# SSD outputs computed by channels, the gate listed behind the next group's x, and part of the attention's scaling on another engine

## The chip, the cores and the metric

The kernel runs on one core of one Trainium2 chip. The metric is the device time of one execution in microseconds; the median of the runs is given, and one execution is recorded by the hardware profiler. The engines are called as the profile calls them: PE (TensorE matmul) with PEld (its weight loads), DVE (VectorE), ACT (ScalarE), POOL (GpSimd) and SP (SyncE, which issues the DMAs).

## The reference

One layer of a hybrid decoder, for 256 positions and a model width of 2048, in f32:

```python
a_in = _rmsnorm(h, attn_norm_g[i])
proj = a_in @ w_in[i]
z, xbc, dt_raw, q, k, v = jnp.split(proj, [o1, o2, o3, o4, o5], axis=-1)
xbc = jax.nn.silu(_causal_dwconv(xbc, conv_w[i], conv_b[i]))
...
y = _ssd(xs_h, dt, a_neg, bm.reshape(b, s, SSM_GROUPS, SSM_STATE),
         cm.reshape(b, s, SSM_GROUPS, SSM_STATE))
y = y + d_skip[i].astype(jnp.float32)[:, None] * xs_h.astype(jnp.float32)
y = y.reshape(b, s, SSM_INNER) * jax.nn.silu(z.astype(jnp.float32))
y_ssm = _rmsnorm(y.reshape(b, s, SSM_GROUPS, SSM_INNER // SSM_GROUPS),
                 ssm_norm_g[i].reshape(SSM_GROUPS, SSM_INNER // SSM_GROUPS))
...
y_att = _swa_sinks(qh, kh, vh, sinks[i])
h = h + jnp.concatenate([y_ssm, y_att], axis=-1) @ w_out[i]
u = _rmsnorm(h, ffn_norm_g[i]) @ w_up[i]
u = _causal_dwconv(u, ffn_conv_w[i], ffn_conv_b[i])
g_ff, u_ff = jnp.split(u, [D_FF], axis=-1)
h = h + (jax.nn.silu(g_ff) * u_ff) @ w_down[i]
gate = jax.nn.sigmoid(_rmsnorm(h, ple_norm_g[i]) @ w_ple_gate[i])
pe = _rmsnorm(p[i] @ w_ple_proj[i], ple_post_g[i])
h = h + gate * pe
```

The SSD part has 32 heads of 64 channels in 4 groups; attention has 32 heads, 8 key heads and a window of 128. In `_ssd`, with L = exp of the masked differences of the cumulated decay inside a chunk, the output of a chunk is (C Bᵀ · L) X plus exp(decay) · C · state of the chunk before. There are two chunks (128 positions each), so only the second has a state before it.

## The kernel before

**Products.** Every large product runs in a split form: weights come by DMA in chunks `w` of 128 x 1024 (two k slices of 512 columns), ACT casts the chunk to `wh` (L192), DVE forms the remainder `wl` (L193), and PE multiplies three times (L222 to L224: high by high, low by high, high by low) for each of the two blocks of 128 positions. A chunk is 12 matmuls of 128x512. The sums lie in PSUM as acc pairs, one tile per block, and each of the two tiles has two buffers: a third pair can start only when the first has been read.

**The SSD phase.** A first phase computes B, C and dt (dt's product is copied by ACT to `dtT`, L379, behind a cast and ahead of the evacuations of B, `ct`, L390). Then for each of four groups of 512 channels: `ssd_x` computes x, makes the decay tiles `seg` (128x1024, two per group, broadcast by DMA from `scr`; then subtraction on DVE, mask on POOL, exp on ACT, times C Bᵀ on DVE) and the group's output y by positions (L533: per head one 128x64 matmul; L537: the state's part, scaled on DVE and added). There are three `seg` buffers. `ssd_gate` computes z with Silu. `ssd_end` multiplies, sums squares on ACT, scales by 1/rms (`ry`), transposes `yc` on PE (L272) and splits it into `yT`, the left side of the output projection. `project` (for group 0) or `output` (groups 1 to 3, in the attention phase) multiplies `yT` with its rows of `w_out` in four quarters of 512 columns and adds each acc to the residual `h` on DVE (L397).

**The order.** Each engine works through its own stream in order. In the SSD phase the streams are laid out when the program is built, by a scheduler that starts from the order of the calls in the code; so small products stand between the matmuls of weight chunks. In the attention phase the order on PE is by hand: a list of parts (q, keys, v, outputs) is run chunk by chunk, each a slot, and the table `at` says at which slot `scores` and `values` are issued. `scores` computes masked scores, exp on ACT, the sum `den`, and scales the probabilities `s` by its reciprocal on DVE (L753) before they are transposed by ACT and POOL copies around a DMA transpose.

**Names.** `ms` are two PSUM tiles for small products, `tr` two for transposes; `prev` is the first chunk's state, copied from PSUM by ACT (L527); `rx` is 1/rms of the input.

Of the kernel before, what the change touches and what calls it, by code (L numbers as in the profile page):

```python
# [11 lines left out]
F32 = mybir.dt.float32  # L12
# [53 lines left out]
def hybrid_layer(  # L66
# [251 lines left out]
    with xin_:  # L318
# [59 lines left out]
        V.tensor_copy(rx, rx_)  # L378
        S.copy(dtT, dt_ps[:64, :T])  # L379

# [12 lines left out]

    def add_to_h(acc, n):
        for b in range(NB):
            hs = hres[b][:, n * NC : (n + 1) * NC]
            V.tensor_tensor(out=hs, in0=hs, in1=acc[b], op=ALU.add)  # L397

# [11 lines left out]

    def project(lhs, w, i0, ni, after=None):

        for n in range(4):
            acc = acc_pair()
            gemm(acc, lhs, [w[i, n] for i in range(i0 * KG // KW, (i0 + ni) * KG // KW)])
            add_to_h(acc, n)
            if after:
                after(n)
# [3 lines left out]
    with tc.tile_pool(name="ssd", bufs=1) as sp, tc.tile_pool(name="dram", bufs=1, space=bass.MemoryType.DRAM) as dp:  # L422
        BT = sb(sp, [P, 4, T], "BT")
        CT = sb(sp, [P, 4, T], "CT")
        for c, (acc, dst, tag) in enumerate(((acc_b, BT, "ct"), (acc_c, CT, "Xd"))):
            t = evac_scaled(acc, sp, tag, 1)
            conv_chunk(t, dst, scw, 4, 16 + 4 * c)
            S.activation(out=dst, in_=dst, func=AF.Silu)
# [42 lines left out]
        nc.sync.dma_start(scr, acsT)  # L471
        eacs = sb(sp, [P, 64], "eacs")
        S.activation(out=eacs, in_=acs, func=AF.Exp)

        def ssd_x(g):
            segs = []
            for c in range(NB):
                hs = slice(g * 16 + c * 8, g * 16 + c * 8 + 8)
                seg = sb(sp, [P, 8, P], "seg", bufs=3)
                nc.sync.dma_start(seg, scr[hs, :].partition_broadcast(P))  # L480
                if c == 0:
                    dec = sb(sp, [P, 8], "dec", bufs=2)
                    V.tensor_tensor(out=dec, in0=seg[:, :, P - 1], in1=acs[:, hs], op=ALU.subtract)
                    S.activation(out=dec, in_=dec, func=AF.Exp)
                V.tensor_tensor(out=seg, in0=seg, in1=bc(acs[:, hs], P), op=ALU.subtract)
                G.affine_select(
                    out=seg, in_=seg, compare_op=ALU.is_ge, fill=-1.0e30, base=0, pattern=[[0, 8], [1, P]], channel_multiplier=-1
                )
                S.activation(out=seg, in_=seg, func=AF.Exp)
                segs.append(seg)  # L490
# [19 lines left out]
            S.activation(out=xc, in_=xc, func=AF.Silu)  # L510
            y, Xd = [], []
            for b in range(NB):
                tr = tr_tile()
                for f in range(4):
                    PE.transpose(tr[:, f * P : (f + 1) * P], xc[:, f, b * P : (b + 1) * P], ident)
                yc = sb(sp, [P, NC], f"yc{b}", bufs=2)
                V.tensor_tensor(out=v3(yc, 8), in0=v3(tr, 8), in1=bc(dsk[:, g * 8 : (g + 1) * 8], HD), op=ALU.mult)
                y.append(yc)
# [8 lines left out]
            S.copy(prev, st)  # L527
            for c in range(NB):
                yc = y[c]
                yp = ms_tile()  # L530
                for h in range(8):
                    hs = slice(h * HD, (h + 1) * HD)
                    PE.matmul(yp[:, hs], lhsT=segs[c][:, h, :], rhs=Xd[c][:, hs], start=True, stop=True)  # L533
                V.tensor_tensor(out=yc, in0=yc, in1=yp, op=ALU.add)
                if c:
                    off = ms_tile()
                    PE.matmul(off, lhsT=CT[:, g, c * P : (c + 1) * P], rhs=prev, start=True, stop=True)  # L537
                    t = sb(sp, [P, NC], "xe")
                    o = g * 16 + 8
                    V.tensor_tensor(out=v3(t, 8), in0=v3(off, 8), in1=bc(eacs[:, o : o + 8], HD), op=ALU.mult)  # L540
                    V.tensor_tensor(out=yc, in0=yc, in1=t, op=ALU.add)
            return y

        def ssd_gate(g):
            acc = in_chunk(3 + 2 * g)
            zs = []
            for b in range(NB):
                z = sb(sp, [P, NC], f"z{b}")
                S.activation(out=z, in_=acc[b], func=AF.Silu, scale=rx[:, b : b + 1])
                zs.append(z)  # L550
            return zs

        def ssd_end(g, y, zs):
            ssy = sb(sp, [P, NB], "ssy", bufs=2)
            for b in range(NB):
                V.tensor_tensor(out=y[b], in0=y[b], in1=zs[b], op=ALU.mult)
                S.activation(out=zs[b], in_=y[b], func=AF.Square, accum_out=ssy[:, b : b + 1])
            ry = rstd(ssy, NC, NB, "ry")
            for b in range(NB):
                V.tensor_scalar_mul(y[b], y[b], ry[:, b : b + 1])  # L560
            yT = Lhs(yp_, KG, "y")
            transpose_split(y, yT, 0, g_ssm[:, 4 * g : 4 * g + 4])
            return (yT, w_out, g, 1)

        y = ssd_x(0)
        zs = ssd_gate(0)

# [69 lines left out]
    with tc.tile_pool(name="att_s", bufs=2) as as_, tc.tile_pool(name="att", bufs=2, reuse_waits="tile") as ap_, tc.tile_pool(name="ps_sc", bufs=1, space=PSUM) as ps_sc:  # L637
# [4 lines left out]

        def turned(table, gain, tag):

            t = sb(as_, [P, NB, HALF], tag, bufs=1)
            V.tensor_tensor(out=t, in0=table, in1=gain.unsqueeze(1).to_broadcast([P, NB, HALF]), op=ALU.mult)
            return t


        qa, qc = qscaled[:, :HALF], qscaled[:, HALF:ROPE]  # L650
        qrope = [turned(t, g, f"qr{i}") for i, (t, g) in enumerate(((cos_t, qa), (sin_t, qc), (cos_t, qc), (sin_t, qa)))]
        krope = [cos_t, sin_t, cos_t, sin_t]
        kgain = sb(as_, [P, HD], "kgs", bufs=1)
# [3 lines left out]
        def norm_rope(acc, b, rope, gain=None):  # L657
            r = sb(ap_, [P, NC], "qkr")
            S.activation(out=r, in_=acc[b], func=AF.Copy, scale=rx[:, b : b + 1])
            n = sb(small, [P, NC], "hsq")  # L660
            S.activation(out=n, in_=r, func=AF.Square)
            ss = sb(as_, [P, 8], "ss8")
            V.tensor_reduce(out=ss, in_=v3(n, 8), axis=AX.X, op=ALU.add)
            rs = rstd(ss, HD, 8, "rs8")
            r3 = v3(r, 8)
            V.tensor_tensor(out=r3, in0=r3, in1=bc(rs, HD), op=ALU.mult)
            if gain is not None:
                G.tensor_tensor(out=r3, in0=r3, in1=gain.unsqueeze(1).to_broadcast([P, 8, HD]), op=ALU.mult)
            a, c_ = r3[:, :, :HALF], r3[:, :, HALF:ROPE]
            t = [sb(as_, [P, 8, HALF], f"rot{i}", bufs=1) for i in range(4)]  # L670
            for i, u_ in enumerate((a, c_, c_, a)):
                G.tensor_tensor(out=t[i], in0=u_, in1=rope[i][:, b, :].unsqueeze(1).to_broadcast([P, 8, HALF]), op=ALU.mult)
            G.tensor_tensor(out=a, in0=t[0], in1=t[1], op=ALU.subtract)
            G.tensor_tensor(out=c_, in0=t[2], in1=t[3], op=ALU.add)
            return r
# [45 lines left out]
        def scores(j, b, kvs):  # L721
# [30 lines left out]
            V.reciprocal(den, den)  # L752
            V.tensor_tensor(out=s, in0=s, in1=bc(den, W), op=ALU.mult)  # L753
            p = s.rearrange("p h w -> p (h w)")
# [4 lines left out]
        def values(j):  # L759

            yT = Lhs(yp_, KG, "y")
            for b in range(NB):
# [15 lines left out]
                split(v3(o, 4), hi, lo)  # L778
            held[4 + j] = (yT, w_out, 4 + j, 1)

# [9 lines left out]
        def output(i):  # L790
            lhs, w, i0, ni = held.pop(i)
            for n in range(4):
                acc = acc_pair()
                for s in range(2):
                    products(acc, lhs, load_w(w[i0 * 2 + s, n]), s * KW, KW, KG, s == 1)
                    if s == 1:
                        add_to_h(acc, n)
# [14 lines left out]
        with tc.manual_schedule(engines={PE.engine}):  # L812
            for part in (
                lambda: q(0),
                lambda: chunk(10, keys),
                lambda: chunk(11, load_v),
# [174 lines left out]
```

## Time and profile before

| | |
|---|---|
| median of three runs | 1434.09 us (1433.94 to 1434.67) |
| the profiled execution | 1435.11 us, of which the span in the trace is 1433.4 us |
| DMA | 292.62 MB, mean 204 GB/s |
| weight splits on DVE, L193 | 495 times, 639.8 us in all |
| casts of weights on ACT, L192 | 495 times, 515.0 us in all |
| adds to h on DVE, L397 | 112 times, 72.8 us in all |

An engine's busy time is the sum of its instructions; matmuls overlap in the array, so a matmul's duration (390 ns for a 128x512) is longer than the step from one to the next. Idle time is put down to the event that ended it, behind an arrow: `<-DVE wl L193` is an instruction that waited for DVE's line 193.

### The profile page before, as it was taken

What the parts mean: (1) busy time and instruction counts of PE and PEld (TensorE: products, weight loads), DVE (VectorE), ACT (ScalarE), POOL (GpSimd) and SP (SyncE); (2) the same over time, 40 slices, a digit from 0 to 9 for tenths busy, and PEclk for the clock granted to TensorE, in tenths of its full rate; (3) what the DMA queues carried; (4) which work ended last, traced back from release to release, by engine and by line L of the source; (5) the groups of instructions that cost most, each with busy time, mean ns of one, the idle gap of its engine ahead of it and who ended that gap; (6) DMA issues with size and microseconds to landing.
All of it is one profiled execution on the core that took longest, in us unless ns stands there. A gap on an engine that the chain in (4) does not pass through costs nothing.

```text
span 1433.4 us, 18075 instructions
## 1 busy us (share of the span) xinstructions
PE 1422.4 (99%) x6527; PEld 1166.0 (81%) x6527; DVE 997.2 (70%) x1242; ACT 792.4 (55%) x1069; POOL 290.5 (20%) x234
## 2 busy tenths in 40 slices
PE   9999999999999999999999999999999999999998
PEld 7888888888777777888888888888888888888887
DVE  7678876776789889756667646665675577476854
ACT  6675555645566655556556446545554554455643
POOL 0002010018434422013243113202320131120000
PEclk9999999999999999999999999999999999999999
DMA  9655665557787877568787767867876876776672
GB/s 341 230 175 209 204 182 185 162 160 207 192 224 201 207 208 221 173 203 213 215 231 201 215 203 209 222 200 203 225 209 195 221 217 201 205 208 190 210 224 65
DMA packets 163466, 292.62 MB, mean 204 GB/s; under 512 B 93040, under 2 KB 95920, under 8 KB 162992
## 3 DMA queue, kind: packets, MB, share of 16 engines
q1 hardware_dynamic: 162944, 290.99, 70.1%
q8 instruction: 51, 0.84, 0.3%
q10 hardware_dynamic: 432, 0.48, 0.1%
q14 instruction: 39, 0.32, 0.1%
HBM read 268.32 MB, written 2.13 MB: 189 GB/s over the span
## 4 chain that ended last, share of the span: by engine, by line
PE 65%; DVE 3%; issue 1%; DMA 1%; ACT 0%; DVEq 0%; SPq 0%; ACTq 0%
PE acc L222 21%; PE acc L223 21%; PE acc L224 21%; DVE wl L193 2%; PE tr L769 1%; PE tr L272 0%; PE sc L732 0%; DMA flip<-half 0%; DVE h L397 0%; DVE s L736 0%; DVE nm L743 0%; ACT wh L192 0%; DMA w<-in_w_in_dram 0%; DVE den L751 0%; DVE sg L921 0%
## 5 line engine op out<-in xcount | busy, mean ns | idle before, releaser
L193 DVE TENSOR_TENSOR wl<-w,wh 128x1024 fp32r<-128x1024 f32 (+1 forms) x495 | 639.8, 1298 | 371.5 <-ACT wh L192 370.5
L192 ACT CAST wh<-w 128x1024 fp32r<-128x1024 f32 (+1 forms) x495 | 515.0, 1045 | 488.9 <-PE acc L224 438.1
L223 PE MATMUL acc<-wl,ah 128*128 128x512 f32 x1278 | 499.8, 391 | 0.6 <-DVE wl L193 0.6
L224 PE MATMUL acc<-wh,al 128*128 128x512 f32 x1278 | 498.7, 390 | 0.0
L222 PE MATMUL acc<-wh,ah 128*128 128x512 f32 x1278 | 498.1, 391 | 0.1
L223 PEld LDWEIGHTS acc<-wl,ah 128*128 128x128 f32 x1278 | 240.0, 188 | 51.4 <-DVE wl L193 1.4
L222 PEld LDWEIGHTS acc<-wh,ah 128*128 128x128 f32 x1278 | 240.0, 188 | 51.4 <-issue 1.4
L224 PEld LDWEIGHTS acc<-wh,al 128*128 128x128 f32 x1278 | 239.9, 188 | 50.2 <-issue 0.7
L224 PE MATMUL acc<-wh,gl 128*128 128x512 f32 x352 | 137.0, 389 | 0.0
L223 PE MATMUL acc<-wl,gh 128*128 128x512 f32 x352 | 137.0, 389 | 0.0
L222 PE MATMUL acc<-wh,gh 128*128 128x512 f32 x352 | 136.4, 389 | 0.0
L871 POOL COPY half<-u 128x1024 uint16<-128x1024 uint16 x44 | 60.2, 1379 | 263.0 <-ACT u L869 262.9
L222 PE MATMUL acc<-wh,yh 128*128 128x512 f32 x256 | 101.4, 396 | 0.6 <-DVE h L397 0.6
L223 PE MATMUL acc<-wl,yh 128*128 128x512 f32 x256 | 99.9, 390 | 0.7 <-DVE wl L193 0.7
L224 PE MATMUL acc<-wh,yl 128*128 128x512 f32 x256 | 99.6, 390 | 0.0
L874 POOL COPY uc<-flip 128x1024 uint16<-128x1024 uint16 x44 | 58.8, 1337 | 177.5 <-DMA flip<-half 177.5
L223 PEld LDWEIGHTS acc<-wl,gh 128*128 128x128 f32 x352 | 66.1, 188 | 13.7
L224 PEld LDWEIGHTS acc<-wh,gl 128*128 128x128 f32 x352 | 66.1, 188 | 13.6
L222 PEld LDWEIGHTS acc<-wh,gh 128*128 128x128 f32 x352 | 66.1, 188 | 13.6
L397 DVE TENSOR_TENSOR h<-h,acc 128x512 f32<-128x512 f32 x112 | 72.8, 679 | 1.1 <-PE acc L224 1.1
L288 DVE SCALAR_TENSOR_TENSOR cv<-uc,fcw,cv 128x254 f32<-128x254 f32 (+1 forms) x176 | 73.0, 476 | 0.0
L222 PEld LDWEIGHTS acc<-wh,yh 128*128 128x128 f32 x256 | 48.0, 188 | 14.3 <-issue 3.8
(236 smaller groups left out, 1126.7 us busy)
## 6 DMA issues: line engine op xcount, KB each, us to landing
w<-in_w_up_dram SPq DMA_DIRECT2D x176, 512.0 KB, 4.0
w<-in_w_in_dram SPq DMA_DIRECT2D x126, 512.0 KB, 4.2
w<-in_w_down_dram SPq DMA_DIRECT2D x88, 512.0 KB, 4.2
w<-in_w_out_dram SPq DMA_DIRECT2D x64, 512.0 KB, 4.3
w<-in_w_pg_dram SPq DMA_DIRECT2D x32, 512.0 KB, 4.1
seg<-scr SPq DMA_DIRECT2D x8, 512.0 KB, 5.0
xt<-in_xT_dram SPq DMA_DIRECT2D x16, 128.0 KB, 7.3
h<-in_x_dram SPq DMA_DIRECT2D x2, 1024.0 KB, 8.6
```

The costliest lines, as they stand in the source:

```text
L192: S.copy(hi, src)
L193: V.tensor_tensor(out=lo, in0=src, in1=hi.bitcast(F32), op=ALU.subtract)
L222: PE.matmul(acc[b], lhsT=hi, rhs=wh[:, i, :], start=(k == 0), stop=False)
L223: PE.matmul(acc[b], lhsT=hi, rhs=wl[:, i, :], start=False, stop=False)
L224: PE.matmul(acc[b], lhsT=lo, rhs=wh[:, i, :], start=False, stop=(k == total - 1 or (b == NB - 1 and k + 1 == whole)))
L288: V.scalar_tensor_tensor(out=dst[:, s:], in0=ps[:, : T - s], scalar=taps[n - 1 - s], in1=dst[:, s:], op0=ALU.mult, op1=ALU.add)
L397: V.tensor_tensor(out=hs, in0=hs, in1=acc[b], op=ALU.add)
L769: PE.matmul(v3(o[e * HD : (e + 1) * HD, kv * 2 * P : (kv + 1) * 2 * P], 2), lhsT=v[kb][:, vs], rhs=pT[e][:, :, kb, :], start=(kb == 0), st ...
L871: G.tensor_copy(half.rearrange("p (a n) -> p a n", a=2), u_.bitcast(U16).rearrange("p (n a) -> p a n", a=2))
L874: G.tensor_copy(uc[:, :, b * P : (b + 1) * P].bitcast(U16).rearrange("p f (t a) -> p f t a", a=2), flip.rearrange("p (a f) t -> p f t a", ...
```

## The change

1. The copy of `dtT` is listed behind the first two evacuations.
2. y is computed by channels: per group 24 matmuls of 64x128 (a head's 64 channels by 128 positions), the two heads of a pair in the two halves of the array's columns. The state's part is accumulated in the same PSUM tile, from `prev` and a new tile `grown` = exp(decay) · C (one exp and one product of 128x1024 per group). The skip term is added on DVE by four scalar_tensor_tensor of 128x256. y needs no transposes; z does, by POOL copies and DMA transposes for groups 0 to 2, and by eight PE transposes for group 3.
3. `ry` is no longer applied to y. The sum of squares is taken over channels by products with ones (two per group), and `ry` becomes a scale in `add_to_h`: h = acc · ry + h.
4. `ssd_end(g)` is listed behind `ssd_x(g + 1)`, and the gate of g + 1 behind it.
5. Rope uses merged tables: four POOL operations per norm_rope instead of six; the keys' gain moves to DVE.
6. In the second block of positions, the probabilities are scaled by ACT, head by head, instead of by one DVE product (eight of the twelve `scores`).
7. The keys' chunk comes ahead of q(0), and `scores` and `values` have other slots.

```diff
     def add_to_h(acc, n, scale=None):
+
         for b in range(NB):
             hs = hres[b][:, n * NC : (n + 1) * NC]
-            V.tensor_tensor(out=hs, in0=hs, in1=acc[b], op=ALU.add)
+            if scale is None:
+                V.tensor_tensor(out=hs, in0=hs, in1=acc[b], op=ALU.add)
+            else:
+                V.scalar_tensor_tensor(out=hs, in0=acc[b], scalar=scale[:, b : b + 1], in1=hs, op0=ALU.mult, op1=ALU.add)
...
+                else:
+                    grown = sb(sp, [P, 8, P], "grown")
+                    S.activation(out=grown, in_=seg, func=AF.Exp)
+                    V.tensor_tensor(
+                        out=grown, in0=grown, in1=CT[:, g, P:].unsqueeze(1).to_broadcast([P, 8, P]), op=ALU.mult
+                    )
...
+            y = sb(sp, [P, 4, T], "y", bufs=2)
+            for half in range(2):
+                yp = ms_tile().rearrange("p (a t) -> p a t", a=2)
+                own = [(0, i, Xd[0], segs[0]) for i in range(2)]
+                for i in range(2):
+                    own += [(1, i, Xd[1], segs[1]), (1, i, prev, grown)]
+                for c, i, left, right in own:
+                    for e_ in range(2):
+                        h = 4 * half + 2 * i + e_
+                        PE.matmul(
+                            yp[e_ * HD : (e_ + 1) * HD, i, c * P : (c + 1) * P],
+                            lhsT=left[:, h * HD : (h + 1) * HD],
+                            rhs=right[:, h, :],
+                            start=(left is not prev),
+                            stop=(left is not Xd[1]),
+                            skip_group_check=True,
+                        )
+                for i in range(2):
+                    f = 2 * half + i
+                    V.scalar_tensor_tensor(
+                        out=y[:, f, :], in0=xc[:, f, :], scalar=skip[:, 4 * g + f : 4 * g + f + 1], in1=yp[:, i, :], op0=ALU.mult, op1=ALU.add
+                    )
...
+            sq = z if g < 3 else sb(sp, [P, 4, T], "zT")
+            S.activation(out=sq, in_=y, func=AF.Square)
+            V.tensor_tensor(out=sq[:, :2, :], in0=sq[:, :2, :], in1=sq[:, 2:, :], op=ALU.add)
+            s1 = sb(sp, [P, T], "ysum")
+            V.tensor_tensor(out=s1, in0=sq[:, 0, :], in1=sq[:, 1, :], op=ALU.add)
+            ps = ms_tile()
             for b in range(NB):
-                V.tensor_scalar_mul(y[b], y[b], ry[:, b : b + 1])
...
+                PE.matmul(ps[:, b : b + 1], lhsT=s1[:, b * P : (b + 1) * P], rhs=ones, start=True, stop=True)
+            return yT, w_out, g, 1, rstd(ps[:, :NB], NC, NB, f"ry{g}")
...
         for g in range(4):
-            held[g] = ssd_end(g, y, zs)
+            y_next = ssd_x(g + 1) if g < 3 else None
+            held[g] = ssd_end(g, y, z)
+            y = y_next
             if g < 3:
-                y = ssd_x(g + 1)
-                zs = ssd_gate(g + 1)
+                z = ssd_gate(g + 1)
             if g < 1:
-                project(*held.pop(g))
+                lhs, w, i0, ni, scale = held.pop(g)
+                project(lhs, w, i0, ni, scale=scale)
...
-            V.tensor_tensor(out=s, in0=s, in1=bc(den, W), op=ALU.mult)
+            if b:
+                for h in range(2 * m):
+                    S.activation(out=s[:, h, :], in_=s[:, h, :], func=AF.Copy, scale=den[:, h : h + 1])
+            else:
+                V.tensor_tensor(out=s, in0=s, in1=bc(den, W), op=ALU.mult)
...
-        for j, first, value in ((0, (30, 33, 36), 50), (1, (43, 46, 51), 65), (2, (58, 61, 66), 79), (3, (75, 77, 80), 93)):
+        for j, first, value in ((0, (28, 31, 34), 48), (1, (43, 46, 50), 64), (2, (58, 61, 65), 79), (3, (75, 77, 80), 93)):
```

How the streams look at the place where the first output projection meets the SSD work of the following groups is shown by rows of the built programs. A row is line, operation, result `<-` operands, size, and how often; numbers behind the names tell buffers apart.

On DVE, in the first output projection of the kernel before, the adds to `h` (L397) stand between weight splits (L193) and the convolution of the next group's x (L288):

```order
L193 TENSOR_TENSOR wl_1672<-w_1670,wh_1671 128x1024
L288 SCALAR_TENSOR_TENSOR xc_1343<-tr_1357,scw_138,xc_1343 128x255
L288 SCALAR_TENSOR_TENSOR xc_1343<-tr_1357,scw_138,xc_1343 128x254
L193 TENSOR_TENSOR wl_1694<-w_1692,wh_1693 128x1024
L397 TENSOR_TENSOR h_1_83<-h_1_83,acc_305_1610 128x512
L288 SCALAR_TENSOR_TENSOR xc_1343<-tr_1357,scw_138,xc_1343 128x253
L397 TENSOR_TENSOR h_2_84<-h_2_84,acc_306_1611 128x512
L193 TENSOR_TENSOR wl_1712<-w_1710,wh_1711 128x1024
L193 TENSOR_TENSOR wl_1791<-w_1789,wh_1790 128x1024
L397 TENSOR_TENSOR h_1_83<-h_1_83,acc_313_1650 128x512
```

The same place on DVE in the changed kernel, with what each row waits for on other engines (`seg_1764` and `seg_2195` are decay tiles of later groups):

```order
L560 SCALAR_TENSOR_TENSOR y_1380<-xc_1332,skip_666,ms_1396 128x256 [waits PE_49]
L185 TENSOR_SCALAR rs_t_1429<-ms_1426 128x2 [waits PE_49]
L512 TENSOR_TENSOR seg_1754<-seg_1754,ms_1774 128x1024 [waits PE_49]
L498 TENSOR_TENSOR grown_1766<-grown_1766,CT_568 128x1024 [waits Activation_49]
L501 TENSOR_TENSOR seg_1764<-seg_1764,acs_658 128x1024 [waits DMAHW0_49]
L493 TENSOR_TENSOR dec_2197<-seg_2195,acs_658 128x8 [waits DMAHW1_49,DVE_49]
L400 SCALAR_TENSOR_TENSOR h_1_83<-acc_302_1594,ry_268_1431,h_1_83 128x512 [waits Pool_49]
L400 SCALAR_TENSOR_TENSOR h_2_84<-acc_303_1595,ry_268_1431,h_2_84 128x512
L400 SCALAR_TENSOR_TENSOR h_1_83<-acc_310_1634,ry_268_1431,h_1_83 128x512
L400 SCALAR_TENSOR_TENSOR h_2_84<-acc_311_1635,ry_268_1431,h_2_84 128x512
```

The adds of the first two quarters now stand together, behind the work on the decay tiles of the next groups.

On PE in the changed kernel, after the last matmul of the projection's second quarter (acc_311) and up to the first of its third (acc_318), rows that repeat left out:

```order
L519 MATMUL tr_1779<-ident_117,BT_567 128x128
L538 MATMUL ms_1376<-xe_1374,Bt_1180 128x512
L550 MATMUL ms_1381<-seg_1153,Xd_254_1365 64x128 x4
L550 MATMUL ms_1381<-seg_1163,Xd_256_1372 64x128 x2
L550 MATMUL ms_1381<-grown_1165,prev_1378 64x128 x2
L550 MATMUL ms_1396<-seg_1153,Xd_254_1365 64x128 x4
L550 MATMUL ms_1396<-grown_1165,prev_1378 64x128 x2
L609 MATMUL ms_1426<-const-float32-1.0,ysum_1424 128x1 x2
L510 MATMUL ms_1774<-CT_568,BT_567 128x128 x2
L222 MATMUL acc_318_1674<-wh_1677,yh_263_1412 128x512
```

Before, the corresponding products (L525, L533, L537) lay between the matmuls of the next group's gate and x, behind the projection:

```order
L222 MATMUL acc_343_1788<-wh_1808,ah_18_141 128x512
L525 MATMUL ms_1391<-xe_1389,Bt_1191 128x512
L533 MATMUL ms_1395<-Xd_258_1378,seg_1167 128x64 x8
L223 MATMUL acc_343_1788<-wl_1809,ah_18_141 128x512
L224 MATMUL acc_343_1788<-wh_1808,al_19_142 128x512
```

All of group 1's y, the ones products of group 0 and the C Bᵀ of group 2 have moved in between two quarters of the projection.

On ACT, at the end of the first phase, before:

```order
L192 CAST wh_751<-w_750 128x1024
L379 COPY hsq_151<-ms_158 64x256
L390 ACTIVATE ct_102_570<-acc_29_152,rx_150 128x512
L390 ACTIVATE ct_103_572<-acc_30_153,rx_150 128x512
L390 ACTIVATE Xd_106_601<-acc_31_154,rx_150 128x512
```

and in the changed kernel:

```order
L192 CAST wh_755<-w_754 128x1024
L389 ACTIVATE ct_102_569<-acc_29_152,rx_150 128x512
L389 ACTIVATE ct_103_571<-acc_30_153,rx_150 128x512
L431 COPY hsq_151<-ms_158 64x256
L389 ACTIVATE Xd_106_601<-acc_31_154,rx_150 128x512
```

The copy (here by the name of the buffer it shares, hsq) now stands behind both evacuations of B.

More of the change, by code (lines that the diff above doesn't have):

```diff
@@ L527, in ssd_x @@
             S.copy(prev, st)
[L528 to L541, printed above, removed]
+            y = sb(sp, [P, 4, T], "y", bufs=2)
[5 more added lines that the diff above has]
+                for c, i, left, right in own:
+                    for e_ in range(2):
+                        h = 4 * half + 2 * i + e_
[12 more added lines that the diff above has]
+                    )
             return y
```

99 lines of the change are left out of this document (61 added, 38 removed).

## The prediction

> **What bounds the kernel now.** I read the page first, then the windows, the groups by shape, and the timelines of the places that the change touches.
>
> ```profile
> span 1433.4 us, 18075 instructions
> PE 1422.4 (99%) x6527; PEld 1166.0 (81%) x6527; DVE 997.2 (70%) x1242; ACT 792.4 (55%) x1069; POOL 290.5 (20%) x234
> PE 65%; DVE 3%; issue 1%; DMA 1%; ACT 0%; DVEq 0%; SPq 0%; ACTq 0%
> 100.00:320.00 220.00, 220.00 (x1074) 182.50 (x1073) 163.78 (x222) 123.47 (x163) 16.86 (x14) 1.00 0.58 183
> 700.00:800.00 100.00, 100.00 (x443) 82.81 (x442) 67.45 (x77) 57.07 (x69) 34.58 (x20) 1.00 0.80 221
> 440.00:460.00 20.00, 19.40 (x88) 15.26 (x88) 19.83 (x24) 12.59 (x19) 12.06 (x16) 1.00 0.75 187
> 510.00:530.00 20.00, 18.80 (x97) 14.85 (x95) 15.55 (x20) 11.92 (x25) 5.15 (x3) 1.00 0.86 233
> 538.00:556.00 18.00, 16.65 (x72) 13.18 (x72) 17.48 (x21) 11.43 (x19) 5.33 (x2) 1.00 0.62 165
> ```
>
> The bound is PE's stream. In the windows (columns: PE, PEld, DVE, ACT, POOL busy, then clock), 443 matmuls fill 100 us at 700 to 800, so one 128x512 matmul is issued every 0.226 us. All of the SSD work lies at 100 to 320 us, where PE never pauses. The attention windows show it idle for 0.60 + 1.20 + 1.35 = 3.15 us. So time changes in two ways only: PE work that goes or comes, and waits of PE that go or come. Other engines count where they make PE wait.
>
> **The SSD products, on PE.** The rows below are timeline rows (start, duration); a step's cost is from its start to the next row's start.
>
> ```profile
> 182.18 1.02 PE L525 MATMUL ms<-xe,Bt 128*128 128x512 f32 x2
> 183.03 1.90 PE L533 MATMUL ms<-Xd,seg 128*128 128x64 f32 x16
> 184.74 0.47 PE L223 MATMUL acc<-wl,ah 128*128 128x512 f32 x1
> 187.13 1.89 PE L533 MATMUL ms<-Xd,seg 128*128 128x64 f32 x16
> 188.86 1.08 PE L537 MATMUL ms<-prev,CT 128*128 128x512 f32 x2
> 190.01 0.40 PE L222 MATMUL acc<-wh,ah 128*128 128x512 f32 x1
> 143.21 1.04 PE L272 MATMUL tr<-ident,yc 128*128 128x128 f32 x8
> 144.00 0.48 PE L223 MATMUL acc<-wl,ah 128*128 128x512 f32 x1
> 413.71 1.16 PE L732 MATMUL sc<-kT,qT 64*128 64x128 f32 x16
> 414.80 0.50 PE L222 MATMUL acc<-wh,ah 128*128 128x512 f32 x1
> 435.35 2.81 PE L769 MATMUL tr<-s,v 128*64 128x256 f32 x24
> 195.47 0.60 PE L494 MATMUL ms<-CT,BT 128*128 128x128 f32 x4
> 195.83 0.48 PE L222 MATMUL acc<-wh,ah 128*128 128x512 f32 x1
> ```
>
> An f32 matmul is two records. Removed per group: y 1.71 + 1.73, off 190.01 - 188.86 less one 0.226 slot = 0.92, transposes of yc 0.79. That is 5.15, or 20.6 over four groups.
>
> Added per group are 24 matmuls, 48 records of 128 columns, in alternating halves of the array's columns. A record of y costs 1.71 / 16 = 0.107. No row shows this shape. The nearest are the values, also in column halves, with 2.81 / 24 = 0.117 per 256-column record where a whole-array record needs 0.85 / 4 = 0.213 for as many (from L525): a ratio of 0.55. The scores, in row halves, give 1.09 / 16 = 0.068, against 0.107: 0.64. I take 0.6: 48 x 0.107 x 0.6 = 3.1, or 12.3 for four; the bounds are half (10.3) and no sharing at all (20.5). [...]
>
> Also added: four clusters of ones products (four records each; L494's four take 0.36, so 1.6 with their entries), the eight transposes of z in the last group (0.9), and two more interruptions in groups 2 and 3, where the y cluster is split (0.4). Sum on PE: -20.6 + 12.3 + 1.6 + 0.9 + 0.4 = **-5.4** (bounds -7.4 and +2.8).
>
> **The moved dtT copy.**
>
> ```profile
> 52.69 1.05 ACT L192 CAST wh<-w 128x1024 fp32r<-128x1024 f32 x1 [0.31 <-PE acc L329]
> 54.31 1.26 ACT L390 ACTIVATE ct<-acc,rx 128x512 f32<-128x512 f32 x2
> 55.09 0.41 PE L299 MATMUL tr<-ident,ct 128*128 128x128 f32 x2 [1.09 <-ACT ct L390]
> ```
>
> PE's transpose waits 1.09 for the ct evacuation, which stood behind the copy. Ahead of it, it can start when the cast ends, 53.74 instead of 54.31: **-0.55** (0 to -1.09). The copy then delays only dt's chain, which PE reaches later.
>
> **The new wait, in the first output projection.** This is the term that decides. Before, its adds to h needed nothing but acc. Now they need ry, whose sum of squares goes through PE (ones(0)); the order puts that behind all of the next group's x on PE, and puts the adds on DVE behind the next groups' seg work. PE cannot start the projection's third quarter (acc_318) before the first quarter's add has freed its acc pair.
>
> ```profile
> seg<-scr SPq DMA_DIRECT2D x8, 512.0 KB, 5.0
> DMA to landing us min/median/max: 3.8/5.0/7.4
> L484 ACT ACT_TABLE_LOAD x1 | 1.3, 1283 | 0.0
> L489 ACT ACTIVATE seg<-seg 128x1024 f32<-128x1024 f32 x8 | 8.5, 1061 | 16.2 <-POOL seg L486 16.1
> L485 DVE TENSOR_TENSOR seg<-seg,acs 128x1024 f32<-128x1024 f32 x8 | 9.7, 1221 | 8.0 <-DMA seg<-scr 8.0
> L397 DVE TENSOR_TENSOR h<-h,acc 128x512 f32<-128x512 f32 x112 | 72.8, 679 | 1.1 <-PE acc L224 1.1
> L527 ACT COPY prev<-ms 128x512 f32<-128x512 f32 x4 | 2.3, 582 | 2.8 <-PE ms L525 2.8
> L187 POOL TENSOR_TENSOR ry<-rs_t,nhalf 128x2 f32<-128x2 f32 x4 | 3.7, 925 | 59.9 <-DVE rs_t L185 59.9
> ```
>
> Clock from the end of the second quarter's matmuls. PE runs Bt's transpose and st to 1.0; the copy of prev (0.58) makes it wait, by my estimate, 0.4 in the middle of the y cluster, which ends near 4.4. Its last read of seg_1153 is at about 3.75. SP issues seg_1764 into that buffer only then (three seg buffers); it lands 5.0 later, 8.75. ACT's table load waits for that landing, 1.28, then exp of grown 1.06: 11.1. DVE stands at grown x CT, as large as seg - acs, 1.22 (12.3), then seg - acs itself, 1.22 (13.5), and only then the add to h: 0.68 (14.2). With 0.4 allowed for dec's few columns and the handovers between engines, PE resumes at 14.6. Without the wait it would have gone on after ones(0) and cb, 0.36 each and 0.1 of entry, at 5.2. So 9.4, and 0.4 for prev: **+9.8**. ry itself is ready earlier (rs_t and the 0.93 on POOL, at about 6.5). With the least and greatest landing, 3.8 and 7.4, it is 8.6 and 12.2; POOL's copies of z beside DVE may add 1. If the add came first after ry, it would be ready at 7.3: a stall near 2.5 is the lower bound.
>
> **The clock after it.** PE then stands still for about 8.5 us.
>
> ```profile
> 1428.00:1430.00 2.00, 0.17 (x2) 1.00 0.29 103
> 1430.00:1433.40 3.40, 0.00 (x0) 0.64 0.27 93
> 0.84 4.39 PE L155 MATMUL ms<-const-bfloat16-1.0 128*128 128x512 bf16 x12 [0.84 <-PEq L981]
> ```
>
> At the end, PE idle since 1428, the granted clock falls to 0.64 on average of the last 3.4 us. At the start, after idleness, twelve 128x512 matmuls take 4.39 us, 0.366 each, against 0.226 later: 12 x 0.140 = 1.7 lost. I take **+1.5** (0 to 1.7). [...]
>
> **DVE beside the SSD work.**
>
> ```profile
> 160.00:180.00 20.00, 20.00 (x94) 16.64 (x93) 18.21 (x27) 8.90 (x9) 0.00 (x0) 1.00 0.57 185
> 454.58 4.16 DVE L193 TENSOR_TENSOR wl<-w,wh 128x1024 fp32r<-128x1024 f32 x2
> ```
>
> DVE is 91% busy there, and twelve POOL copies of z are new beside it; these two splits, beside POOL copies, took 4.16 where L485 needs 1.22 for as many elements. One late split in the first quarter of the projection: **+0.5** (0 to 2).
>
> **Attention.**
>
> ```profile
> L753 DVE TENSOR_TENSOR s<-s,den 128x1024 f32<-128x1024 f32 x12 | 14.9, 1244 | 0.3
> L747 ACT ACTIVATE s<-s,nm 128x256 f32<-128x256 f32 x32 | 15.9, 498 | 19.0 <-DVE nm L744 18.9
> PE sc L732 <- DVE s L736: 1.2, 1, 1.2
> ```
>
> Eight of twelve s x den go from DVE (1.24 each) to ACT (4 x 0.50). In 440:460 and 538:556 DVE was busy for 19.83 of 20 and 17.48 of 18 us, so it was the late one; those 1.95 us of idleness are relieved. The 1.2 of 510:530 waits for s on DVE; an earlier slot may move it either way. 24 of the 32 scaled adds fall here too; against 0.68 I price them as the same. Rope's merged tables and kgain shift work off POOL, which is 20% busy: nothing. Taken **-1.5** (all waits gone -3.15; one ACT block of 2.0 exposed, +2). The keys' chunk first costs nothing: the same matmuls in another order.
>
> **Sum:** -5.4 - 0.55 + 9.8 + 1.5 + 0.5 - 1.5 = +4.35. Against the profiled execution's 1435.11 (span 1433.4 and 1.7 around it) that is 1439.5; that execution lay 1.0 above the median of the runs, so on 1434.09: **1438.4**.
>
> **Rivals.**
> [...]
> - *The stall is near mine, but it is repaid elsewhere*: the clock does not fall (-1.5) and the attention waits go whole (-1.65): +1.2, **1435.3**, not to be told from no change. For it: DVE gets 10 us back in attention.
> - *Column halves do not share the array*: 48 x 0.107 per group, +8.2 on my sum, **1446.6**. Against it: the row of the values.
>
> **How the numbers follow.** Forecast 0.45, its own range 1435.5 to 1442.5 (stall 8.6 to 12.2, attention and DVE at either end); short wait 0.17; repaid 0.25; no sharing 0.13. About 0.2%, 2.9 us, is what a measurement of this kernel can tell from no change. Faster takes nearly all of the short wait and a little of the repaid case, 0.17; same takes most of the repaid case and the forecast's low edge, 0.28; slower the rest, 0.55. The range takes in the short wait's centre and stops short of the third rival: 1428 to 1444.
>
> **What would show it.** In the profile after: PE's longest wait, some 9 us, on DVE's h in the first projection near 170 us, with DVE waiting on ACT's grown and ACT on seg's DMA; a granted clock below 1 there. 48 records of y per group in about 3.1 us. The 1.09 wait at 55 us halved. Attention's windows with less than 3.15 us idle. Wrong if PE does not pause in the projection, or if y's records start 0.107 apart.

## The result and the profile after

The changed kernel takes 1443.16 us (median of five, 1440.97 to 1445.84) against 1434.67 (1433.94 to 1435.79): a ratio of 1.0058, 95% interval 1.0046 to 1.0069. It is slower by 8.5 us. The forecast was 1438.4 in a range of 1428 to 1444.

The profiled execution took 1441.1 us, of which the span is 1439.4, 6.0 more than before. The head of its page, its chain, and PE's waits (engine and line that waited, what it waited for, total, times, longest):

```profile
span 1439.4 us, 18205 instructions
PE 1418.6 (99%) x6575; PEld 1162.1 (81%) x6575; DVE 990.0 (69%) x1237; ACT 805.8 (56%) x1091; POOL 297.7 (21%) x224
PE 94%; DVE 3%; DMA 1%; issue 1%; ACT 1%; SPq 0%; DVEq 0%; ACTq 0%
```

```profile
PE acc L222 <- DVE h L400: 10.1, 2, 9.8
PE acc L223 <- DVE wl L193: 2.4, 1, 2.4
PE tr L299 <- issue: 0.9, 1, 0.9
```

PE is busy 3.8 us less than before and the span is 6.0 longer; two waits that did not exist, 9.8 and 2.4, explain it, together with the granted clock behind each of them. The windows (PE busy, clock, DMA share, GB/s) around the first and the second wait:

```profile
148.00:150.50 2.50, 0.39 (x2) 0.97 0.01 5
150.50:154.00 3.50, 3.24 (x8) 0.53 0.63 169
154.00:158.00 4.00, 4.00 (x20) 1.00 0.74 235
174.00:184.50 10.50, 0.68 (x4) 0.67 0.64 170
184.50:188.50 4.00, 3.72 (x10) 0.57 0.01 4
188.50:192.00 3.50, 3.50 (x17) 1.00 0.00 0
```

To compare kernels whose work lies at different times, I add up one thing in each trace: every step from one 128x512 matmul to the next that is longer than the usual 0.227, less that 0.227. What is left is small work put in between, waits and half clock. A is the first 100 us, SSD the stretch to 320, attention to 625; later stretches hardly differ.

| kernel | median us | A | SSD | attention |
|---|---|---|---|---|
| before | 1434.67 | 10.6 | 33.2 | 35.2 |
| changed | 1443.16 | 10.4 | 43.7 | 31.4 |
| changed, second profile (again, one execution) | 1445.03 | 10.6 | 45.3 | 32.7 |
| ones_tr | 1436.73 | 10.4 | 36.8 | 33.2 |
| list_before | 1431.44 | 9.9 | 31.7 | 31.6 |
| z0_pe | 1447.32 | 9.7 | 45.3 | 34.4 |
| seg4 | 1436.88 | 10.6 | 37.1 | 33.2 |
| list_seg4 | 1426.60 | 9.7 | 28.1 | 32.2 |
| ls4_noatt | 1429.67 | 9.7 | 28.4 | 34.6 |
| ls4_sden | 1430.63 | 10.4 | 27.5 | 34.6 |
| b_att | 1434.55 | 9.8 | 33.6 | 35.4 |
| b_sden | 1432.59 | 10.7 | 34.1 | 33.0 |
| b_rope | 1435.73 | 9.8 | 33.4 | 36.5 |
| b_slots | 1441.86 | 9.8 | 33.9 | 43.1 |

So the SSD stretch lost 10.5 us and attention won 3.8. The medians of the kernel before lay between 1434.67 and 1435.15 in all groups of runs.

The wait in the projection, step by step (timeline rows: start, duration, engine, and in brackets the idle time and what ended it), first PE, then DVE, then ACT:

```profile
173.18 0.61 PE L609 MATMUL ms<-const-float32-1.0,ysum 128*128 128x1 f32 x4
174.32 0.68 PE L510 MATMUL ms<-CT,BT 128*128 128x128 f32 x4 [0.53 <-DVE rs_t L185]
184.78 0.79 PE L222 MATMUL acc<-wh,yh 128*128 128x512 f32 x1 [9.78 <-DVE h L400]
```

```profile
175.04 1.22 DVE L512 TENSOR_TENSOR seg<-seg,ms 128x1024 f32<-128x1024 f32 x1 [0.80 <-PE ms L510]
180.67 1.23 DVE L498 TENSOR_TENSOR grown<-grown,CT 128x1024 f32<-128x1024 f32 x1 [4.42 <-ACT grown L497]
181.81 2.17 DVE L501 TENSOR_TENSOR seg<-seg,acs 128x1024 f32<-128x1024 f32 x1
183.91 0.15 DVE L493 TENSOR_TENSOR dec<-seg,acs 128x8 f32<-128x8 f32 x1
183.99 2.71 DVE L400 SCALAR_TENSOR_TENSOR h<-acc,ry,h 128x512 f32<-128x512 f32 x4
```

```profile
178.29 1.28 ACT L497 ACT_TABLE_LOAD   x1 [7.28 <-DMA seg<-scr]
179.59 1.06 ACT L497 ACTIVATE grown<-seg 128x1024 f32<-128x1024 f32 x1
```

The reader sees the chain that the order gave in advance: PE ends its small work at 175.0; the seg load, issued at about 172.4 when the y cluster has read its buffer, lands at 178.3; the table load, exp, grown x CT and seg - acs follow one after another (the last took 2.17 instead of 1.22, beside a POOL copy of z); the adds to h begin at 184.0, and 0.8 later PE goes on. Meanwhile ry had been ready since 175.1.

The second wait, at 148 us, is told by the same kind of row some 15 us earlier. First ACT, then two rows of DVE, then PE:

```profile
132.74 1.06 ACT L497 ACTIVATE grown<-seg 128x1024 f32<-128x1024 f32 x1 [3.46 <-DMA seg<-scr]
```

```profile
133.84 1.23 DVE L498 TENSOR_TENSOR grown<-grown,CT 128x1024 f32<-128x1024 f32 x1 [2.89 <-ACT grown L497]
...
149.50 1.21 DVE L193 TENSOR_TENSOR wl<-w,wh 128x1024 fp32r<-128x1024 f32 x1
```

```profile
150.76 0.79 PE L223 MATMUL acc<-wl,ah 128*128 128x512 f32 x1 [2.37 <-DVE wl L193]
151.35 0.63 PE L224 MATMUL acc<-wh,al 128*128 128x512 f32 x1
151.78 0.63 PE L223 MATMUL acc<-wl,ah 128*128 128x512 f32 x1
152.21 0.63 PE L224 MATMUL acc<-wh,al 128*128 128x512 f32 x1
```

DVE stood for 2.89 us for grown of group 1 with weight splits behind it, and worked without a pause from 133.8 on; the split for PE came at 149.5. Behind the wait a matmul starts every 0.43 us instead of 0.227.

### The profile page after: what moved, and what is told of

Same layout as the page of the kernel before. It is cut to its first block, busy times and chain, and to the rows that moved or that the text cites. A ratio compares the mean times of both kernels' runs of the same rounds, so it can differ in the third digit from the quotient of the medians.

```text
span 1439.4 us, 18205 instructions
## 1 busy us (share of the span) xinstructions
PE 1418.6 (99%) x6575; PEld 1162.1 (81%) x6575; DVE 990.0 (69%) x1237; ACT 805.8 (56%) x1091; POOL 297.7 (21%) x224
## 4 chain that ended last, share of the span: by engine, by line
PE 94%; DVE 3%; DMA 1%; issue 1%; ACT 1%; SPq 0%; DVEq 0%; ACTq 0%
PE acc L222 29%; PE acc L223 29%; PE acc L224 29%; PE acc L329 3%; DMA seg<-scr 1%; DVE wl L193 1%; PE sc L786 1%; PE ms L550 1%; PE tr L827 1%; PE tr L272 0%; DMA w<-in_w_in_dram 0%; DVE seg L501 0%; PE tr L299 0%; PE tr L531 0%; PE ms L538 0%
## 5 line engine op out<-in xcount | busy, mean ns | idle before, releaser
L193 DVE TENSOR_TENSOR wl<-w,wh 128x1024 fp32r<-128x1024 f32 (+1 forms) x495 | 636.5, 1291 | 386.0 <-ACT wh L192 384.9
L288 DVE SCALAR_TENSOR_TENSOR cv<-uc,fcw,cv 128x254 f32<-128x254 f32 (+1 forms) x176 | 73.0, 475 | 0.0
L224 PEld LDWEIGHTS acc<-wh,yl 128*128 128x128 f32 x256 | 48.4, 189 | 10.4
```

The source lines that it names most:

```text
L193: V.tensor_tensor(out=lo, in0=src, in1=hi.bitcast(F32), op=ALU.subtract)
L224: PE.matmul(acc[b], lhsT=lo, rhs=wh[:, i, :], start=False, stop=(k == total - 1 or (b == NB - 1 and k + 1 == whole)))
L288: V.scalar_tensor_tensor(out=dst[:, s:], in0=ps[:, : T - s], scalar=taps[n - 1 - s], in1=dst[:, s:], op0=ALU.mult, op1=ALU.add)
```

## The experiments

Each row of the table above is one of them. Those in a first group change one thing in the changed kernel.

**ones_tr**: where ones(0) stands on PE.

```diff
-            ps = ms_tile()
+            ps = tr_tile()
             for b in range(NB):
                 PE.matmul(ps[:, b : b + 1], lhsT=s1[:, b * P : (b + 1) * P], rhs=ones, start=True, stop=True)
```

> Changed kernel, with one word altered: the two products with ones take a buffer of the pool tr instead of ms, so they need not come behind the next group's y. Theory A (PE's 9.8 us wait in the first output projection comes from the order: ones(0) behind group 1's y for want of an ms buffer, so the adds to h stand behind grown and seg on DVE): the wait falls below 1 us, the 1.7 us at half clock after it go too, the 2.4 us wait at 148 us stays; about 11.5 us less than the changed kernel, near 1431.7. Rival B (the late load of seg is the cause and is only met elsewhere): a wait of 5 us or more appears at the next splits or at group 2's y, and the time stays within 3 us of the changed kernel's 1443.

It took 1436.73 (ratio to before 1.0008, 0.9995 to 1.0021): 6.4 less than the changed kernel. PE's waits:

```profile
PE acc L223 <- DVE wl L193: 4.9, 4, 2.4
PE acc L222 <- DVE h L400: 1.7, 3, 0.7
```

The 9.8 us are gone with one word: theory A holds for the place of the wait, and B, which asked for a new wait of 5 us or more, falls. But 11.5 us were expected. Waits for wl of 0.9 and 1.0 came in at 188 and 198 us, one of 0.5 at 147, and one of 0.9 for ACT's ct at 136 (the sum for SSD fell by 6.9), and the wait of 2.4 near 150 stayed, as expected. The seg load still comes late, and DVE still stands for it; only the adds to h no longer stand behind it.

**list_before**: the listing of the calls.

```diff
-            y_next = ssd_x(g + 1) if g < 3 else None
             held[g] = ssd_end(g, y, z)
-            y = y_next
             if g < 3:
+                y = ssd_x(g + 1)
                 z = ssd_gate(g + 1)
```

> Changed kernel with the listing of before: ssd_end(g), then ssd_x(g+1), then its gate. Theory A: ones(0) comes ahead of group 1's y again, the adds to h lie between the weight splits, and both long PE waits (9.8 us in the projection, 2.4 us at 148 us) and the 3.3 us at half clock go: about 15 us less, near 1428. Rival C (the listing was needed to hide the transposes of z by POOL and DMA, some 10 us from the gate to y x zT): ssd_end(g) then waits for z, ACT and DVE wait with it, PE waits 5 us or more in some group, and the time is 1435 to 1441.

It took 1431.44, 0.9977 of before (0.9965 to 0.9988), faster than both kernels. The 9.8 us wait is gone, and of the waits for wl 1.5 us remains, after which the clock did not fall (it is 1.00 over 150 to 156 us). Theory A is borne out, though 15 us were expected and 11.7 came; rival C falls: nothing in PE waited for z. The new listing, by which the products with ones come behind the next group's y, cost 11.7 us by the medians, and all the rest of the change together gains 3.2.

**z0_pe**: z of group 0 transposed on PE.

```diff
-            if g == 3:
+            if g in (0, 3):
                 return zs
...
-            if g < 3:
+            if g not in (0, 3):
                 V.tensor_tensor(out=y, in0=y, in1=z, op=ALU.mult)
...
-            sq = z if g < 3 else sb(sp, [P, 4, T], "zT")
+            sq = z if g not in (0, 3) else sb(sp, [P, 4, T], "zT")
```

> Changed kernel with z of group 0 transposed on PE, as for group 3, without POOL copies and DMA transposes. Theory D (the 2.4 us wait for wl at 148 us comes from POOL: two seg masks stand behind a copy of zT there, ACT's exp of seg waits 2.1 us for them with the casts of weights behind it): the wait goes, and the 1.6 us at half clock after it; PE gets 0.9 us of transposes; 3 us less than the changed kernel, near 1440, and the 9.8 us wait stays. Rival E (the work of ssd_end(0) on DVE and ACT beside x of group 1 is simply too much): the wait stays above 1.5 us, and the time is 1442 to 1445.

It took 1447.32, 4 more than the changed kernel; neither number. The wait for wl went, as D says, and in its place PE waited for the transposes' own chain:

```profile
PE acc L222 <- DVE h L400: 10.8, 4, 8.4
PE tr L597 <- DVE Xd L533: 1.7, 1, 1.7
PE tr L531 <- ACT xc L526: 1.0, 1, 1.0
```

The 8.4 is the wait in the projection, now at 178 us; the other two come within 4 us of each other, at 154 and 157, and in the windows PE's clock is 0.50 from 159 to 163. Since the edit also moved much of ssd_end(0) later, it does not tell D from E; inconclusive.

**again**: a second profile of the changed kernel.

> The changed kernel once more, for a second profile, since its five times spread over 4.9 us. Theory: the two long waits differ from execution to execution (the seg load landed after 5.8 us; 3.8 to 7.4 were seen before), so the wait in the projection lies between 8 and 12 us and the one at 148 us between 1 and 4. Rival: the waits are as in the first profile, and the spread lies in the granted clock or elsewhere.

1445.03, with waits of 9.7 and 2.4 us where the first profile had 9.8 and 2.4. Both lie inside the theory's ranges too, but in these two executions the waits agree within 0.1, so the spread lies elsewhere, as the rival has it; two profiles do not show that the waits never vary. Of the 3.9 us that this span is longer, SSD has 1.6 and attention 1.3 in the table above. In SSD it is mostly the half clock: 18 steps of 0.43 us between matmuls against 11, 1.0 of the 1.6.

**seg4**: four seg buffers.

```diff
-                seg = sb(sp, [P, 8, P], "seg", bufs=3)
+                seg = sb(sp, [P, 8, P], "seg", bufs=4)
...
-        adt = sb(sp, [P, 64], "adt")
+        adt = sb(sp, [P, 64], "dt_e1")
...
-        acs = sb(sp, [P, 64], "acs")
+        acs = sb(sp, [P, 64], "dt_l1")
```

> Changed kernel with four seg buffers instead of three (two small tiles share buffers to make room). Theory F (both long PE waits have one root: a seg load can be issued only when the y cluster has read its buffer, and what waits for it stands at the head of DVE's and ACT's streams): near 130 us DVE no longer waits 2.9 us for grown, so the 2.4 us wait for wl at 148 us goes with its 1.6 us of half clock. In the projection the adds still stand behind dec, which waits for the load of seg_2195 into the buffer that the y cluster frees, but no longer behind a table load, exp and grown that begin only at a landing: that wait falls from 9.8 to about 7. Together about 6.5 less than the changed kernel, near 1437. Rival E (too much DVE work beside x of group 1): the wait at 148 us stays above 1.5, time near 1440.

It took 1436.88 (1.002, 1.0011 to 1.0029). PE's longest waits, DVE where it stood for grown before, and DVE in the projection:

```profile
PE acc L222 <- DVE h L400: 6.7, 3, 5.7
PE ms L510 <- DVE rs_t L185: 1.1, 1, 1.1
```

```profile
128.26 1.22 DVE L498 TENSOR_TENSOR grown<-grown,CT 128x1024 f32<-128x1024 f32 x1 [0.22 <-ACT grown L497]
...
130.53 1.22 DVE L193 TENSOR_TENSOR wl<-w,wh 128x1024 fp32r<-128x1024 f32 x1
134.59 0.53 DVE L493 TENSOR_TENSOR dec<-seg,dt_l 128x8 f32<-128x8 f32 x1 [2.83 <-DMA seg<-scr]
```

```profile
172.22 1.22 DVE L498 TENSOR_TENSOR grown<-grown,CT 128x1024 f32<-128x1024 f32 x1
...
175.12 0.63 DVE L493 TENSOR_TENSOR dec<-seg,dt_l 128x8 f32<-128x8 f32 x1 [0.55 <-DMA seg<-scr]
...
177.94 2.72 DVE L400 SCALAR_TENSOR_TENSOR h<-acc,ry,h 128x512 f32<-128x512 f32 x4
```

No wait of PE for wl is left, and the one in the projection is 5.7 instead of 9.8 (7 were expected). So the late load at the head of a stream has a part in both waits, as theory F says, but it is not all of either. In the projection DVE waits only 0.55 for a load; the 5.7 that is left is its own seg work, 172.2 to 177.9, listed ahead of the adds. At 130 us the wait for grown is gone, but DVE now stands 2.83 for the next load, at dec: in the 26.3 us from the end of x (123.2 in the changed kernel, 124.3 here) it is idle for 3.1 instead of 5.5. The streams were also laid out anew: the split that PE waited for now comes ahead of four rows of yl and one of zT, not behind them. What the earlier load gives and what the new place gives is not separated here. Rival E, that the work on DVE alone makes the wait, falls, since that work is still there.

**list_seg4**: both edits, the former listing and four seg buffers.

> The listing of before and four seg buffers in the changed kernel. Theory F: the 1.5 us wait for wl at 153 us, which stayed with the former listing, goes too, since DVE's 5.8 us of waiting for grown at 130 to 136 us goes; about 1.5 to 2 us less than the former listing alone (1431.4), near 1429.5. Rival E: it stays, 1431 to 1432.

1426.60, 0.9951 of before (0.9938 to 0.9965): the fastest of all, 16.6 us below the changed kernel. PE's waits:

```profile
PE tr L299 <- issue: 0.9, 1, 0.9
PE acc L222 <- DVE h L400: 0.6, 1, 0.6
PE acc L223 <- DVE wl L193: 0.4, 1, 0.4
```

The gain over list_before is 4.8, more than the 1.5 to 2 expected; the SSD sum fell by 3.6, so besides the 1.5 for wl smaller waits went too.

The second group takes the attention part apart. **b_att** is the kernel before with the whole attention part of the change (the diff's parts from the rope tables on, but without the scale in the adds), **b_sden** with the ACT scaling alone, **b_slots** with the keys' chunk first and the slots alone, **b_rope** with the merged tables and the keys' gain alone.

```diff
-            V.tensor_tensor(out=s, in0=s, in1=bc(den, W), op=ALU.mult)
+            if b:
+                for h in range(2 * m):
+                    S.activation(out=s[:, h, :], in_=s[:, h, :], func=AF.Copy, scale=den[:, h : h + 1])
+            else:
+                V.tensor_tensor(out=s, in0=s, in1=bc(den, W), op=ALU.mult)
```

> Kernel before with only the attention part of the change: merged rope tables, keys' gain on DVE, ACT scaling of the second block, keys' chunk first, the new slots. By the trace of the changed kernel the attention part gives 3.8 us (12 score clusters 15.27 to 13.98, other gaps 5.58 to 3.03): 1431 against 1434.7. By my prediction it gives 1.5: 1433.2. If it gave nothing by itself (the gain came from work that the SSD part took off DVE there), 1434.7.

> Kernel before with only the scaling of the second block's probabilities moved from DVE to ACT. My prediction's reason (the waits near 455, 545 and 554 us end with DVE, which loses 1.24 us per block): these three waits go, 1.5 to 2.4 us less. Rival (the slots and the keys' place did it): nothing, or up to 1 us more, where ACT's 2 us per block delay casts.

> Kernel before with only the keys' chunk first and the new slots. My prediction held that the keys' place costs nothing and that an earlier slot may move the 1.2 us wait for s either way: 1433.5 to 1436. If the slots are what took back the 2 us in the kernel of before with the whole attention part: 1436.5 to 1437.5.

> Kernel before with only the merged rope tables and the keys' gain on DVE. My prediction put these at nothing, since POOL is 20% busy: 1434.5 to 1435.7. If they took back the 2 us (a 128x512 product more on DVE per block of keys, longer POOL operations beside DVE): 1436.5 to 1437.5; if POOL was late for q after all: 1433 to 1434.

b_att: 1434.55, 0.9998 (0.9990 to 1.0007), nothing, and its attention sum is that of before. b_sden: 1432.59, 0.9984 (0.9976 to 0.9993); the three waits behind the scaling at 455, 545 and 554 us are gone, as the prediction's reason has it, and one of 1.6 for POOL's qT has come. b_rope: 1435.73, 1.0006 (0.9997 to 1.0015), not to be told from nothing. b_slots: 1441.86, 1.0053 (1.0040 to 1.0066), more than 4 us beyond both expectations. Its own trace says why (first PE's waits, then POOL):

```profile
PE sc L732 <- POOL qT L683: 5.4, 2, 4.7
```

```profile
364.07 1.04 POOL L695 COPY half<-qkr 128x1024 uint16<-128x1024 uint16 x1
372.70 1.15 POOL L683 COPY qT<-flip 128x1024 uint16<-128x1024 uint16 x1 [7.59 <-DMA flip<-half]
```

With the keys first, q(0) is ready eight slots later and the first scores are asked for two slots earlier; POOL's last copy of q is then late by 4.7 us. The clock falls during that wait too: it is 0.84 over 368 to 373.5 us and 0.50 over 373.5 to 378.5, where PE, back at 373.9, is busy for 4.60 us, which costs about 2.3: together the 7 us. In b_att, where rope is four POOL operations instead of six, that wait is 1.1. So the slots, taken alone, lose by asking for q too early; with the merged tables and the ACT scaling beside them the loss is gone.

**ls4_sden** and **ls4_noatt** take the attention part out of list_seg4, wholly or up to the ACT scaling.

> The fastest version so far (former listing and four seg buffers, 1426.6) with the attention part of before except the scaling on ACT: no merged rope tables, no keys' gain on DVE, q(0) ahead of the keys, former slots. If the rest of the attention part costs the 2 us by which the two kernels of before with attention edits differ (1434.55 against 1432.59): 1424.6. If the rest helps once the SSD part is changed: 1428 or more. If it does neither: 1426 to 1427.

> The same version with the whole attention part of before. By the traces the attention stretch lost 35.2 us to small work and gaps before and 32.2 in that version: 3 us more than 1426.6, near 1429.7. If the attention part gives as little here as in the kernel before (0.6 by the medians): near 1427.

ls4_noatt: 1429.67, 0.9968 (0.9956 to 0.9981), as the traces had it. ls4_sden: 1430.63, 0.9970 (0.9958 to 0.9982): the ACT scaling without the rest gives nothing here. In list_seg4 the whole attention part is worth some 3 us by the medians (the intervals of the two ratios overlap; the attention sums differ by 2.4), and in the kernel before nothing that can be told from zero. What in the SSD part makes the difference stays open; neither the scaled adds nor the state in which the SSD stretch leaves the queues was tried by itself.

## Why the prediction was right, and where its sizes were off

The direction, the place and the mechanism came out as forecast. The size did not: 8.5 us were lost where 4.35 were forecast, and 1443.16 lies in the stated range but above the forecast's own, 1435.5 to 1442.5. By its terms:

- **The SSD products on PE, -5.4.** The SSD sum of the changed kernel is 43.7; without the waits of 9.8 and 2.4 and the 3.1 of half clock it is 28.4, against 33.2: -4.8. list_seg4, which has almost no waits, shows 28.1. The column halves do share the array: 48 records in 2.77 us from the first row below to the last, 0.058 each, against 0.107 for a whole-array record. The rival without sharing is out. At 2.77 instead of 3.1 the y products gave 1.3 more than forecast in four groups, and yet the sum is 0.6 short, so PE's other small work is some 2 us off; which piece was not taken apart.

```profile
123.23 0.88 PE L550 MATMUL ms<-seg,Xd 128*64 128x128 f32 x12
...
125.68 0.39 PE L550 MATMUL ms<-grown,prev 128*64 128x128 f32 x4
126.00 0.50 PE L224 MATMUL acc<-wh,al 128*128 128x512 f32 x1
```

- **The new wait, +9.8.** Measured 9.8. The links differ a little and cancel: the load took about 5.9 instead of 5.0 and one subtraction 2.17 instead of 1.22, while PE's own small work ended 0.6 later than I had it. That the size agrees so well is in part luck; the 0.4 for prev did not come, and PE waited 0.5 for rs_t instead. ones_tr, list_before and seg4 show that the two conditions named in the prediction, ones(0) behind the y cluster and the adds behind the seg work, carry it: take away the first and it goes; bring the load earlier and it shrinks to 5.7, which is the seg work itself.

- **The clock, +1.5.** It fell as forecast, during this wait (0.67 over 174.0 to 184.5 us), and was 0.57 over the 4 us behind it. That it would fall in the middle of the kernel, and how long the half rate would last, was my estimate; no run had shown it, and none shows the 1.5 for this wait. The slow steps behind it cost 1.6 in the first profile; in the second there were four more of them, 2.4 in all. It fell once more, in the wait at 148 us, for 1.5, which I had not; that pause was 2.37 us.

- **DVE beside the SSD work, +0.5 (0 to 2). This is the term that was mis-sized.** I priced one late split from DVE's work and POOL's copies. It measured 2.4 of wait and 1.5 of half clock, 3.9 together, outside my bounds. What I had not counted is the same chain as in the projection, one group earlier: grown of group 1 waits for a seg load that group 0's y had held back, and the splits stand behind it. I had followed that chain at one of its places only; it stands at each group's turn. POOL may have a part too, as I had it: while it copied zT and masked two seg tiles, 136.2 to 142.5 us, a subtraction and a split at 137 to 141.5 us took 2.19 and 2.10 instead of 1.22; but the split ahead of them, beside the same copy, took 1.22. Nor need that make the wait alone: in seg4 the slowest subtraction took 2.19 as well, and PE waited for no wl. How the 2.4 divide between the load, POOL's work and the place of the split in the stream stays open.

- **The moved dtT copy, -0.55.** Measured -0.2: ct's evacuation could not start at the end of the cast; PE's dt products ended its wait.

```profile
53.73 1.26 ACT L389 ACTIVATE ct<-acc,rx 128x512 f32<-128x512 f32 x2 [0.35 <-PE ms L336]
```

- **Attention, -1.5.** Measured -3.8 in the first profile and -2.5 in the second. Since the work lies some us later than before, the short windows of the prediction do not hold the same work any more; from 320 to 640 us PE is idle for 0.36 us in the first profile and 1.17 in the second, against 3.23 before.

My reason for it, that DVE was the late one there, holds in b_sden. That the keys' place and rope cost nothing by themselves does not: b_slots loses 7 us, which the rest of the attention part makes good.

Together the terms of the first profile are -4.8 - 0.2 + 9.8 + 1.6 + 3.9 - 3.8 = +6.5, where its span is 6.0 longer. Two misses of opposite sign, 3.4 too little for DVE and 2.3 too little gain in attention, partly cancel in it. The median is a further 2.5 above that span's difference, because the first profiled execution was one of the two fastest of five, and the kernel before's a little slow; again, with 4 us more, shows that the half clock and attention vary from one execution to the next. The rivals of a short wait (a stall near 2.5) and of a repaid one are out: the wait is as long as forecast, attention repaid more than I took, and the second wait took it back.

## What to carry to other kernels

When the order puts a load whose buffer comes free late ahead of work that the bound engine needs, price the whole stream behind it (landing, table load, exp, product, and only then the needed row), and look for the same chain at every turn of the loop, not only where it is longest. A small PSUM tile from a rotating pool ties its user to whatever was listed before it: here one word, the pool that the products with ones take their buffer from, was worth 6 us, and the listing 12. Edits to a schedule belong together with those that made room for them: the slots lost 7 us alone, and nothing together with the faster rope and the ACT scaling.

## What the runs showed of the hardware that was not expected

PE's clock was halved not only in the long wait, where I had it, but also after a step of 2.76 us from one matmul to the next (a pause of 2.37). In the changed kernel's trace it is 0.50 from 150.37 to 153.78 us and from 177.67 to 187.91, for 3.41 and 10.24 us; at full rate it stood for 23.89 us between the two and for 1249.28 behind them, up to 1437.19. These four lengths are 1, 3, 7 and 366 times 3.413 us. Windows of that length (PE busy, clock, DMA share, GB/s), first in the changed kernel, then in its second profile, then in z0_pe:

```profile
146.95:150.37 3.42, 1.44 (x7) 1.00 0.28 113
150.37:153.78 3.41, 3.02 (x7) 0.50 0.52 155
153.78:157.20 3.42, 3.42 (x16) 1.00 0.74 207
...
150.74:154.16 3.42, 1.49 (x6) 1.00 0.11 19
154.16:157.57 3.41, 3.41 (x9) 0.50 0.86 255
...
153.56:156.97 3.41, 1.16 (x9) 1.00 0.80 275
```

In the 3.41 us ahead of these falls PE was busy for 1.44, 1.49 and 1.16 us, and ahead of the fall at 177.67 in the changed kernel for 0.68. In z0_pe, where the clock was 0.85 over 152 to 159 us and 0.50 over 159 to 163, no single pause was longer than 1.71 us; one of 1.04 lay ahead of it, with transposes between them. In list_before, whose longest wait there was 1.5 us, PE was busy for 4.39 of the 6 us from 150 to 156, and the clock stayed at 1.00. What decides it was not shown. In the second profile the clock did not fall in the pause itself: PE was busy for 1.32 of the 1.6 us up to 154.0 at a clock of 1.00, and the fall came at 154.16.

In the first profile the half rate ended at 153.78 and 187.91, after 3.02 and 3.13 us of work in it. In z0_pe PE was busy for 2.56 us from 156.97 to 160.38, and the clock was still 0.50 up to 163. Behind a long pause PE worked at half rate for these 3.02 and 3.13 us in the first profile, for about 4.9 behind the long wait of the second (clock 0.53 over 186.5 to 192, PE busy for 5.22 of these 5.5 us), and for at least 4.60 in b_slots; at 0.43 us from one matmul to the next instead of 0.227, about half of that was lost. It varies between executions of the same program: 1.6 and 2.4 us behind the long wait in the two profiles of the changed kernel. Of the ten executions of ones_tr, the two shortest (1433.2 and 1433.5) had a mean granted clock of 1.000, the two longest (1439.6 and 1441.5) one of 0.997.
